# The last normalisation of a two-layer encoder: right half squared about its own mean, passes shared over three engines, three stores at the end

## The chip, the cores and the metric

The kernel runs on one core of a Trainium2 chip. A core has a matrix engine (TensorE, PE in the profile, with its weight loads as PEld), VectorE (DVE), ScalarE (ACT), GpSimd (POOL) and SyncE (SP), which here only issues transfers. Each engine works through its own instructions strictly in order and waits for others by semaphores. SBUF is the on-chip memory of 128 partitions; PSUM holds TensorE's sums. The metric is device time of one execution in microseconds (us).

## The reference

The input x is 1024 tokens by 1024 columns in float32. Two layers are computed: the first mixes tokens by latent attention, the second by differential attention, and each then has a gated feed-forward part. After each part stands a normalisation:

```python
h = _layernorm(ALPHA * h + mix, ln_mix_g[i], ln_mix_b[i])
h = _layernorm(ALPHA * h + _swiglu(h, ffn_w_gu[i], ffn_w_down[i]), ln_ffn_g[i], ln_ffn_b[i])

def _layernorm(x, g, b):
    mu = jnp.mean(x32, axis=-1, keepdims=True)
    var = jnp.mean(jnp.square(x32 - mu), axis=-1, keepdims=True)
    y = (x32 - mu) * lax.rsqrt(var + LN_EPS) * g + b
```

The change concerns the very last of these, behind the feed-forward part of the second layer, for the first 512 tokens.

## The kernel before, in words

Float32 products are made of three matmuls each on numbers split into a high and a low part: the cast to the high part is ScalarE's (`split`, the profile's L470), the subtraction for the low part VectorE's or GpSimd's (L471).

The second half of the function `ffn` multiplies the hidden activations with `w_dn`. It uses a scheme of seven products of half size in place of eight: the 1024 rows are two halves of four row blocks each (128 rows a block), the 1024 columns two halves (`lo_half`, `hi_half`). `whole` runs one of the seven products: 11 steps of the inner dimension, each for four row blocks, into four PSUM tiles of 128x512. `added` (L799) then adds such a PSUM tile to half a row block of `z`, on VectorE, and where it is the last addition to that half, it also leaves the row sums in `sums[block][:, 0]` (left half) or `[:, 1]` (right half).

The upper blocks 4 to 7 are complete after the fifth product and are normalised there by `finish`. The sixth product (`from_h(5, "7")`, `t3`) completes the right half of blocks 0 to 3. The seventh (`from_h(2, "4")`, `t4`) completes their left half; in the last layer (`next_x is None`) it runs blocks 0 and 1 together through the 11 steps, then block 2, then block 3. Its weights are made as it runs: VectorE subtracts (L770), ScalarE casts (L470), GpSimd subtracts (L471), TensorE uses them (L783).

Behind each block, `last(t)` adds the left half and calls `finish`, that is `layer_norm`: two one-column operations on VectorE make minus the mean from the two sums (L167, L168); ScalarE squares both halves of z about the mean and accumulates (L171), writing the squares to a PSUM tile that is free; VectorE forms (z - mean) * g over 1024 columns (L177); VectorE adds the two sums of squares and the epsilon (L179); GpSimd raises that to the power -1/2 (L181); VectorE forms y * rs + b over 1024 columns (L184), in halves for block 3; SyncE stores it (L185), 512 KB a block, two times 256 KB for block 3.

The instructions are written block by block; a compiler that simulates time puts them in the order in which each engine gets them, an earlier line first where several are ready. The small columns (means, sums, powers) come from one pool of 22 buffers (`small`). Nothing in the change is a matmul.

Of the kernel before, what the change touches and what calls it, by code (L numbers as in the profile page):

```python
# [11 lines left out]
AF = mybir.ActivationFunctionType  # L12
ALU = mybir.AluOpType
# [3 lines left out]
P = 128  # L17
S = 1024
D = 1024
# [11 lines left out]
LN_EPS = 1e-5  # L31
# [11 lines left out]
def trunk(  # L43
# [32 lines left out]
    nc = tc.nc  # L76
    V, A, G, T = nc.vector, nc.scalar, nc.gpsimd, nc.tensor
# [25 lines left out]
    mhalf = cst[:, 0:2]  # L103
# [22 lines left out]
    def small(name, n=1):  # L126
        return sp.tile([P, 2], F32, tag="small", name=name, bufs=22)[:, :n]
# [23 lines left out]
    def bcast_row(pool, src, n, name, tag):  # L151
        t = pool.tile([P, n], F32, tag=tag, name=name, bufs=1)
        nc.gpsimd.dma_start(t, src.partition_broadcast(P))
        return t
# [6 lines left out]
            reason="kept in program order",  # L161
        )

    def layer_norm(z, sums, junk, y, g, b, name, dst, n=1):

        nmu = small(f"nmu_{name}", 2)
        V.tensor_scalar(nmu[:, 0:1], sums[:, 0:1], sums[:, 1:2], -1.0 / (32 * D), ALU.add, ALU.mult)  # L167
        V.tensor_scalar(nmu[:, 1:2], sums[:, 0:1], sums[:, 1:2], -1.0 / D, ALU.add, ALU.mult)  # L168
        ssq = small(f"ssq_{name}", 2)
        squares = [  # L170
            A.activation(  # L171
                junk[i], z[:, i * 512:(i + 1) * 512], AF.Square,
                bias=nmu[:, 0:1], scale=1.0 / 32, accum_out=ssq[:, i:i + 1],
            )
            for i in range(2)
        ]
        centred = V.scalar_tensor_tensor(y, z, nmu[:, 1:2], g, ALU.add, ALU.mult)  # L177
        ve = small(f"ve_{name}")
        V.tensor_scalar(ve, ssq[:, 0:1], ssq[:, 1:2], LN_EPS, ALU.add, ALU.add)  # L179
        rs = small(f"rs_{name}")  # L180
        G.tensor_tensor(rs, ve, mhalf[:, 0:1], ALU.pow)  # L181
        for i in range(n):
            c = slice(i * D // n, (i + 1) * D // n)
            V.scalar_tensor_tensor(y[:, c], y[:, c], rs, b[:, c], ALU.mult, ALU.add)  # L184
            nc.sync.dma_start(dst[:, c], y[:, c])  # L185
        return squares[0].ins, centred.ins

    def to_xT(y, xT, tb, name, where):
# [90 lines left out]
    def out_proj(side, w_o, o_dram, x_src, x_dst, lng, lnb, xo):  # L279


        with tc.tile_pool(name="op0", bufs=2, side=side, reuse_waits="tile") as pool:
# [13 lines left out]
            for tb in LAST_ORDER:  # L296
                nm = f"a0_{tb}"
                of = pool.tile([P, H, P], F32, tag="of", name=f"of_{nm}", bufs=2)
                src = o_dram[tb // 2][:, :, (tb % 2) * P:(tb % 2) * P + P]
                nc.sync.dma_start(of, src.rearrange("h p q -> p h q"))  # L300
                ot = pool.tile([P, 2, D], F32R, tag="oh", name=f"oh_{nm}").rearrange("p a (h q) -> p a h q", h=H)
                oh, ol = ot[:, 0], ot[:, 1]
                A.copy(oh, of)
                V.tensor_tensor(ol, of, f32(oh), ALU.subtract)
                zy = pool.tile([P, 2, D], F32, tag="zy", name=f"zy_{nm}")
                z, y = zy[:, 0], zy[:, 1]
                nc.sync.dma_start(z, x_src[tb * P:(tb + 1) * P, :])
                sums = small(f"sum_{nm}", 2)
                junk = []
                for nh in range(2):  # L310
                    c = slice(nh * 512, nh * 512 + 512)
                    m = (ps_m if nh == 0 else ps_t)(f"zp_{nm}_{nh}")
                    junk.append(m)
                    mm3(m, [(oh[:, h, :], ol[:, h, :], wo[h][0][:, c], wo[h][1][:, c]) for h in range(H)])
                    V.scalar_tensor_tensor(
                        z[:, c], z[:, c], ALPHA, m, ALU.mult, ALU.add, accum_out=sums[:, nh:nh + 1]
                    )
                if tb == LAST_ORDER[-1]:
                    y = big_tile(f"y_{nm}", F32)[:, 0]
                layer_norm(z, sums, junk, y, g, b, nm, x_dst[tb * P:(tb + 1) * P, :])  # L320
                if prev is not None:
                    raw_x(prev[1], xo, prev[0], f"a0_{prev[0]}")
                prev = (tb, y)
        return lambda: raw_x(prev[1], xo, prev[0], f"a0_{prev[0]}")

    class OutProj:
# [90 lines left out]
        def rest(self, lng, lnb, xo):  # L417
            gb = big_tile("gb1", F32)
            for i, src in enumerate((lng, lnb)):
                nc.gpsimd.dma_start(gb[:, i], src.partition_broadcast(P))  # L420
            prev = None
            for tb in LAST_ORDER:
                if tb not in LAST_ORDER[:2]:
                    self.of(tb)
                if tb != LAST_ORDER[0]:
                    self.late(tb)
                z, y = self.z[tb]
                layer_norm(z, self.sums[tb], [self.m[tb, nh] for nh in range(2)], y, gb[:, 0], gb[:, 1],
                           f"a1_{tb}", self.x_dst[tb * P:(tb + 1) * P, :])
                if prev is not None:  # L430
                    raw_x(self.z[prev][1], xo, prev, f"a1_{prev}")
                prev = tb
            self.st.close()
            return lambda: raw_x(self.z[prev][1], xo, prev, f"a1_{prev}")
# [52 lines left out]
    def ffn(side, xo, xst, pending, layer, x_src, x_dst, lng, lnb, next_x):  # L487
# [3 lines left out]
        nm = f"f{layer}"  # L491
# [212 lines left out]
        z, sums = {}, {}  # L704
        lo_half, hi_half = slice(0, 512), slice(512, 1024)
# [74 lines left out]
        def step(o, h, w, tb, first, last):  # L780
            c = slice(tb * P, (tb + 1) * P)
            for a, b_ in ((0, 0), (0, 1), (1, 0)):
                T.matmul(  # L783
                    o, h[:, a, c], w[:, b_], start=(first and (a, b_) == (0, 0)), stop=(last and a == 1),
                    skip_group_check=True,
                )
# [7 lines left out]
        def rows(half, tb):  # L794
            return tb + 4 - 4 * half

        def added(half, cs, o, tb, acc=None, scale=1.0):
            n = rows(half, tb)
            banks_read.append(V.scalar_tensor_tensor(  # L799
                z[n][:, cs], z[n][:, cs], scale, o, ALU.mult, ALU.add,  # L800
                **({} if acc is None else {"accum_out": sums[n][:, acc:acc + 1]}),
            ).ins)

        def finish(tb, junk, y=None):
            y = z[tb] if y is None else y
            return layer_norm(z[tb], sums[tb], junk, y, g, b, f"{nm}_{tb}", x_dst[tb * P:(tb + 1) * P, :],
                              2 if next_x is None and tb == 3 else 1)

        def accumulators(name, tag):
            if tag == "x":  # L810
                return [ps_s(f"d{name}{layer}_{t}") for t in range(4)]
            return [(ps_m if t < 2 else ps_t)(f"d{name}{layer}_{t}") for t in range(4)]
# [8 lines left out]
        x4, y4 = accumulators("x", "x"), accumulators("y", "y")  # L821
# [3 lines left out]
        g = bcast_row(pool, lng, D, f"fg{layer}", "g")  # L825
        b = bcast_row(pool, lnb, D, f"fb{layer}", "b")
# [20 lines left out]
        y4 = accumulators("w", "y")  # L847
# [4 lines left out]
        x4 = accumulators("v", "x")  # L852
        whole(x4, from_h(6, "3"), block(1, hi_half, "b22"), True)
        for t in range(4):
            added(0, hi_half, x4[t], t, 1)
            finish(4 + t, [x4[t], x4[t]])

        whole(y4, from_h(5, "7"), t3(), False)
        for t in range(4):
            added(1, hi_half, y4[t], t, 1)  # L860

        def last(t):
            added(1, lo_half, y4[t], t, 0)
            finish(t, [y4[t], y4[t]])

        new, rest, normed = None, [], []
        if next_x is None:
            hs, ws = [], []
            for h, w in zip(from_h(2, "4"), t4()):
                hs.append(h)  # L870
                ws.append(w)
                for t in range(2):
                    step(y4[t], h, w, t, False, len(hs) == 11)
            stx.close()
            last(0)
            last(1)
            for t in range(2, 4):
                for j in range(11):
                    step(y4[t], hs[j], ws[j], t, False, j == 10)
                last(t)  # L880
        else:
# [11 lines left out]
            junk = wp.tile([P, 2, 512], F32, tag="wr", name=f"junk_{nm}", bufs=2)  # L893
            for t in range(4):
                y = yb[t // 2][:, t % 2]
# [4 lines left out]
            for t in range(4):  # L900
                y = yb[t // 2][:, t % 2]
# [133 lines left out]
    with ast as st:  # L1035
# [117 lines left out]
        for h in range(1, H):  # L1153
            b = 8 * (h - 1)
# [30 lines left out]
    xo, stacks = x_pools("m0", "right")  # L1185
    pending = out_proj("left", w_o_a, o_dr[0], x, xs_dr[0], ln_mix_g[0], ln_mix_b[0], xo)
    xT, rest, normed = ffn("left", xo, stacks, pending, 0, xs_dr[0], xs_dr[1], ln_ffn_g[0], ln_ffn_b[0], next_x)


    banks("ps3", PS_BUFS_B)  # L1190
    with ExitStack() as st:
# [11 lines left out]
        for ql in q_lo:  # L1203
            for mp in range(2):
                b = slice(64 - mp * 64, 128 - mp * 64)
                z = bb[b, :512]
# [132 lines left out]
        for h in range(1, H):  # L1339
            b = 8 * (h - 1)  # L1340
# [20 lines left out]
        b = 8 * (H - 1) - 2  # L1361
# [12 lines left out]
    pending = proj[0].rest(ln_mix_g[1], ln_mix_b[1], xo)  # L1374
    banks("ps4", PS_BUFS)
    ffn("right", xo, stacks, pending, 1, xs_dr[2], out, ln_ffn_g[1], ln_ffn_b[1], None)
    ps_stack.close()

# [87 lines left out]
```

## Time and profile before

| | |
|---|---|
| median of three runs | 2333.69 us |
| lowest and highest of them | 2331.33 and 2339.92 us |
| profiled execution, first to last instruction | 2331.5 us |
| TensorE busy | 2254.7 us |
| VectorE busy | 1556.9 us |
| ScalarE busy | 1017.4 us |
| GpSimd busy | 894.8 us |

The profiled execution has its span recorded, not a time of its own beside it; the lowest run is 0.1 us below that span and the median 2.2 us above it. In rows of the timeline the first number is the start in us from the span's start, the second the time from the first start to the last end of the instructions merged in that row, then engine, source line, operation, what is written and read, shapes and count; in brackets stands the idle time ahead and what ended it. In grouped rows the two numbers behind the bar are the total busy time in us and the mean of one instruction in ns. In rows with three numbers by slashes these are minimum, median and maximum in ns. A block's normalisation appears under the line numbers given above; `dw` is the PSUM tile of the last product, `wt` its weights.

### The profile page before, as it was taken

What the parts mean: (1) busy time and instruction counts of PE and PEld (TensorE: products, weight loads), DVE (VectorE), ACT (ScalarE), POOL (GpSimd) and SP (SyncE); (2) the same over time, 40 slices, a digit from 0 to 9 for tenths busy, and PEclk for the clock granted to TensorE, in tenths of its full rate; (3) what the DMA queues carried; (4) which work ended last, traced back from release to release, by engine and by line L of the source; (5) the groups of instructions that cost most, each with busy time, mean ns of one, the idle gap of its engine ahead of it and who ended that gap; (6) DMA issues with size and microseconds to landing.
All of it is one profiled execution on the core that took longest, in us unless ns stands there. A gap on an engine that the chain in (4) does not pass through costs nothing. (4 is left out here: it accounts for less than half of the span.)

```text
span 2331.5 us, 31115 instructions
## 1 busy us (share of the span) xinstructions
PE 2254.7 (97%) x11410; PEld 1918.7 (82%) x11410; DVE 1556.9 (67%) x2876; ACT 1017.4 (44%) x2089; POOL 894.8 (38%) x706
## 2 busy tenths in 40 slices
PE   7899999999999999999999999979999999999997
PEld 7898997888888887888888898867788888887885
DVE  4567664596656667677576666666596656658777
ACT  4366664352333333444465656545342333324353
POOL 3233452014444445555432424222014444436564
PEclk9999999999999999999999999989999999999999
DMA  5112324344323238454220212153334323337353
GB/s 201 35 57 89 120 90 161 109 163 153 118 85 131 73 118 320 172 194 153 91 55 19 69 37 69 37 190 101 124 141 151 107 98 106 111 131 303 142 203 118
DMA packets 102490, 288.29 MB, mean 124 GB/s; under 512 B 7856, under 2 KB 30000, under 8 KB 91840
## 3 DMA queue, kind: packets, MB, share of 16 engines
q1 hardware_dynamic: 96480, 267.48, 32.4%
q0 software_dynamic: 5856, 18.81, 2.5%
q8 instruction: 90, 1.47, 0.3%
q14 instruction: 64, 0.52, 0.1%
HBM read 205.00 MB, written 77.07 MB: 121 GB/s over the span
## 5 line engine op out<-in xcount | busy, mean ns | idle before, releaser
L470 ACT CAST op_g<-gr 128x512 fp32r<-128x512 f32 x240 | 147.5, 622 | 410.7 <-PE gb L515 228.1
L471 POOL TENSOR_TENSOR op_g<-gr,op_g 128x512 fp32r<-128x512 f32 x104 | 145.9, 1408 | 303.0 <-DVE tmp L606 153.6
L471 DVE TENSOR_TENSOR op_h<-rh,op_h 128x512 fp32r<-128x512 f32 x154 | 161.4, 1078 | 69.9 <-ACT op_h L470 69.9
L515 PE MATMUL ga<-xh_m,op_g 128*128 128x512 f32 x512 | 168.0, 389 | 0.0
L470 ACT CAST op_h<-rh 128x512 fp32r<-128x512 f32 x154 | 92.9, 619 | 147.7 <-PE dx L783 37.2
L783 PE MATMUL dw<-op_w_t,op_h 128*128 128x512 f32 x660 | 151.4, 390 | 0.2 <-DVE op_h L471 0.2
L783 PEld LDWEIGHTS dw<-op_w_t,op_h 128*128 128x128 f32 x660 | 123.6, 188 | 26.1 <-DVE op_h L471 0.6
L223 ACT ACTIVATE l_b<-l_b,mx_b 128x256 f32<-128x256 f32 (+7 forms) x128 | 99.6, 778 | 76.0 <-DVE mx_b L220 74.3
L1269 POOL TENSOR_SCALAR l_b<-l_b,r_b,cst 128x128 f32<-128x128 f32 (+3 forms) x64 | 52.8, 825 | 204.0 <-DVE r_b L225 194.8
L471 POOL TENSOR_TENSOR op_w_t<-tt,op_w_t 128x512 fp32r<-128x512 f32 x66 | 98.7, 1499 | 78.7 <-ACT op_w_t L470 76.8
L783 PE MATMUL dx<-op_w_b,op_h 128*128 128x512 f32 x528 | 122.6, 391 | 5.9 <-ACT op_w_b L470 3.9
L783 PEld LDWEIGHTS dx<-op_w_b,op_h 128*128 128x128 f32 x528 | 98.4, 188 | 29.8 <-ACT op_w_b L470 4.7
L515 PE MATMUL gb<-t4h_f,op_g 128*128 128x512 f32 x352 | 115.8, 390 | 3.2 <-DVE tmp L598 3.2
L515 PE MATMUL gc<-b22h_f,op_g 128*128 128x512 f32 x352 | 115.6, 389 | 1.0 <-ACT op_g L470 1.0
L471 DVE TENSOR_TENSOR op_g<-gr,op_g 128x512 fp32r<-128x512 f32 x136 | 109.5, 806 | 9.0 <-ACT op_g L470 8.8
L515 PE MATMUL gc<-t1h_f,op_g 128*128 128x512 f32 x352 | 115.5, 389 | 0.0
L515 PE MATMUL gb<-t3h_f,op_g 128*128 128x512 f32 x352 | 115.2, 389 | 0.0
L515 PE MATMUL gb<-t2h_f,op_g 128*128 128x512 f32 x352 | 114.9, 389 | 0.0
L515 PEld LDWEIGHTS ga<-xh_m,op_g 128*128 128x128 f32 x512 | 96.1, 188 | 20.0
L471 POOL TENSOR_TENSOR op_g<-s,op_g 128x512 fp32r<-128x512 f32 x40 | 55.9, 1398 | 142.9 <-ACT op_g L470 142.9
L144 PE MATMUL bp<-xT_f,h_wb 128*128 128x512 f32 x256 | 103.0, 402 | 0.1
L146 PE MATMUL bp<-xT_f,l_wb 128*128 128x512 f32 x256 | 101.6, 397 | 0.0
(381 smaller groups left out, 6788.5 us busy)
## 6 DMA issues: line engine op xcount, KB each, us to landing
gr<-in_w_gu SPq DMA_DIRECT2D x44, 1024.0 KB, 6.6
rh<-h_dr SPq DMA_DIRECT2D x28, 1024.0 KB, 4.9
h_dr<-sh SPq DMA_DIRECT2D x22, 1024.0 KB, 4.9
h_dr<-hp SPq DMA_DIRECT2D x22, 768.0 KB, 4.1
tt<-in_w_dn SPq DMA_DIRECT2D x22, 512.0 KB, 7.6
rh<-h_dr SPq DMA_DIRECT2D x14, 768.0 KB, 4.4
z<-xs_dr SPq DMA_DIRECT2D x16, 512.0 KB, 10.0
rw_b<-in_w_dn SPq DMA_DIRECT2D x8, 1024.0 KB, 8.8
```

Source lines behind the costliest of these rows:

```text
L144: T.matmul(ps_out, lh, rh, start=(i == 0), stop=False)
L146: T.matmul(ps_out, ll, rh, start=False, stop=(i == n - 1))
L223: A.activation(l[:, :n], l[:, :n], AF.Exp, bias=mx, scale=-1.0, accum_out=sm)
L470: A.copy(hi, src)
L471: eng.tensor_tensor(lo, src, f32(hi), ALU.subtract)
L515: T.matmul(o, w[:, a, kc], x[b][:, k, :], start=(first and k == 0 and (a, b) == (0, 0)), stop=(k == 3 and a == 1), skip_group_check=True,)
L783: T.matmul(o, h[:, a, c], w[:, b_], start=(first and (a, b_) == (0, 0)), stop=(last and a == 1), skip_group_check=True,)
L1269: G.tensor_scalar(l1[:, :n], l1[:, :n], r1, nlam, ALU.mult, ALU.mult)
```

## The change

Only the first four row blocks of the last layer's second normalisation are computed otherwise, by `begin_norm` and `end_norm` in place of `finish`.

`begin_norm(t)`, behind the sixth product: one column operation makes minus the mean of the right half alone, ScalarE squares the right half about that mean with a sum, and another column operation adds epsilon to it. `end_norm(t)`, behind the seventh product: ScalarE squares the left half about the same value (the right half's mean); from the two row sums VectorE forms minus the full mean and minus the square of the difference between the full mean and the right half's, with which the sum of squares is corrected to be about the full mean; GpSimd's power follows. For blocks 0 to 2, ScalarE then forms rs * z - rs * mean over 1024 columns, VectorE multiplies by g, GpSimd adds b, and SyncE stores. For block 3, VectorE forms (z - mean) * g in two halves ahead of the power, and y * rs + b in three pieces of 512, 256 and 256 columns behind it, each with its own store; the middle one is issued by ScalarE. `layer_norm` loses its splitting into `n` pieces, which only block 3 used.

```diff
-    def layer_norm(z, sums, junk, y, g, b, name, dst, n=1):
+    def layer_norm(z, sums, junk, y, g, b, name, dst):
...
-        for i in range(n):
-            c = slice(i * D // n, (i + 1) * D // n)
-            V.scalar_tensor_tensor(y[:, c], y[:, c], rs, b[:, c], ALU.mult, ALU.add)
-            nc.sync.dma_start(dst[:, c], y[:, c])
+        V.scalar_tensor_tensor(y, y, rs, b, ALU.mult, ALU.add)
+        nc.sync.dma_start(dst, y)
...
+        def square(t, i, cs, junk):
+
+            A.activation(
+                junk, z[t][:, cs], AF.Square, bias=about[t][0], scale=1.0 / 32, accum_out=about[t][1][:, i:i + 1]
+            )
+
+        def begin_norm(t, junk):
+
+
+            nb, q = small(f"nb{layer}_{t}"), small(f"q{layer}_{t}")
+            about[t] = nb, small(f"sq{layer}_{t}", 2), q
+            V.tensor_scalar(nb, sums[t][:, 1:2], -1.0 / (32 * 512), None, ALU.mult)
+            square(t, 1, hi_half, junk)
+            V.tensor_scalar(q, about[t][1][:, 1:2], LN_EPS, None, ALU.add)
+
+        def end_norm(t, junk):
+
+            s_lo, s_hi = (sums[t][:, i:i + 1] for i in range(2))
+            nb, sq, q = about[t]
+            square(t, 0, lo_half, junk)
+            d, nmu, rs = (small(f"{k}{layer}_{t}", 2) for k in ("dm", "nm", "rs"))
+            V.tensor_scalar(nmu[:, 0:1], s_lo, s_hi, -1.0 / D, ALU.add, ALU.mult)
+            V.tensor_scalar(d[:, 0:1], s_lo, s_hi, 1.0 / D, ALU.subtract, ALU.mult)
+            V.tensor_scalar(d[:, 1:2], d[:, 0:1], d[:, 0:1], -1.0, ALU.mult, ALU.mult)
+            V.tensor_scalar(d[:, 1:2], d[:, 1:2], q, None, ALU.add)
+            y, dst = z[t], x_dst[t * P:(t + 1) * P, :]
+
+            def scale():
+                V.tensor_scalar(rs[:, 1:2], sq[:, 0:1], d[:, 1:2], None, ALU.add)
+                G.tensor_tensor(rs[:, 0:1], rs[:, 1:2], mhalf[:, 0:1], ALU.pow)
+
+            if t < 3:
+                scale()
+                V.tensor_scalar(nmu[:, 1:2], nmu[:, 0:1], rs[:, 0:1], None, ALU.mult)
+                A.activation(y, y, AF.Identity, bias=nmu[:, 1:2], scale=rs[:, 0:1])
+                V.tensor_tensor(y, y, g, ALU.mult)
+                G.tensor_tensor(y, y, b, ALU.add)
+                nc.sync.dma_start(dst, y)
+                return
+            for cs in (lo_half, hi_half):
+                V.scalar_tensor_tensor(y[:, cs], y[:, cs], nmu[:, 0:1], g[:, cs], ALU.add, ALU.mult)
+            scale()
+            for cs, eng in ((lo_half, nc.sync), (slice(512, 768), nc.scalar), (slice(768, 1024), nc.sync)):
+                V.scalar_tensor_tensor(y[:, cs], y[:, cs], rs[:, 0:1], b[:, cs], ALU.mult, ALU.add)
+                eng.dma_start(dst[:, cs], y[:, cs])
...
         for t in range(4):
             added(1, hi_half, y4[t], t, 1)
+            if next_x is None:
+                begin_norm(t, x4[t])
 
         def last(t):
             added(1, lo_half, y4[t], t, 0)
-            finish(t, [y4[t], y4[t]])
+            end_norm(t, y4[t])
```

More of the change, by code (lines that the diff above doesn't have):

```diff
@@ L805, in finish @@
             y = z[tb] if y is None else y
-            return layer_norm(z[tb], sums[tb], junk, y, g, b, f"{nm}_{tb}", x_dst[tb * P:(tb + 1) * P, :],
-                              2 if next_x is None and tb == 3 else 1)
+            return layer_norm(z[tb], sums[tb], junk, y, g, b, f"{nm}_{tb}", x_dst[tb * P:(tb + 1) * P, :])
+        about = {}
+        def square(t, i, cs, junk):
+            A.activation(
+                junk, z[t][:, cs], AF.Square, bias=about[t][0], scale=1.0 / 32, accum_out=about[t][1][:, i:i + 1]
+            )
```

## The prediction

> **What bounds the kernel now.** I read the page first, to see which engine fills the span, then the chain that ended last, then the last 47 us engine by engine.
>
> ```profile
> span 2331.5 us, 31115 instructions
> ...
> PE 2254.7 (97%) x11410; PEld 1918.7 (82%) x11410; DVE 1556.9 (67%) x2876; ACT 1017.4 (44%) x2089; POOL 894.8 (38%) x706
> ```
>
> TensorE is the bound of the whole. The change touches nothing ahead of the last seventh product of the second feed-forward layer, so the question is where TensorE ends and what comes behind it. From the timeline of all engines:
>
> ```profile
> 2290.53 28.90 PE L783 MATMUL dw<-wt,op_h 128*128 128x512 f32 x126 [1.78 <-DVE z L799]
> ```
>
> The last product ends at 2290.53 + 28.90 = 2319.43, without a gap. What is left is a tail of 2331.46 - 2319.43 = 12.0 us, 0.52% of the time. A measurement of this kernel tells about 0.5%, 11.7 us, from no change: the tail would have to vanish for a visible gain. The chain of waits over the end, and the stretches by engine (busy us of PE, weight loads, VectorE, ScalarE, GpSimd, then clock and DMA):
>
> ```profile
> 2319.79 0.69 DVE z L799 x2
> 2320.47 1.20 DVE z L177
> 2321.67 0.14 DVE ve_f L179
> ...
> 2321.88 0.55 POOL rs_f L181
> ```
>
> ```profile
> 2309.50:2319.50 10.00, 9.93 (x44) 7.88 (x42) 7.64 (x18) 4.66 (x11) 1.10 (x2) 1.00 0.14 55
> 2319.50:2327.20 7.70, 0.00 (x0) 0.00 (x0) 6.56 (x12) 1.87 (x6) 1.09 (x2) 0.78 0.33 136
> ```
>
> Behind TensorE's end VectorE is busy 6.56 of 7.70 us: it is the bound of the tail, with GpSimd's power between two of its passes. VectorE's own timeline shows what it does there and what a pass costs:
>
> ```profile
> 2289.79 0.68 DVE L799 SCALAR_TENSOR_TENSOR z<-z,dw 128x512 f32<-128x512 f32 x1
> ...
> 2291.60 0.68 DVE L799 SCALAR_TENSOR_TENSOR z<-z,dw 128x512 f32<-128x512 f32 x1
> ...
> 2309.49 0.69 DVE L799 SCALAR_TENSOR_TENSOR z<-z,dw 128x512 f32<-128x512 f32 x1 [3.49 <-PE dw L783]
> ...
> 2310.79 0.21 DVE L167 TENSOR_SCALAR nmu_f<-fs 128x1 f32<-128x1 f32 x1
> 2310.91 0.20 DVE L168 TENSOR_SCALAR nmu_f<-fs 128x1 f32<-128x1 f32 x1
> ...
> 2312.73 1.28 DVE L177 SCALAR_TENSOR_TENSOR z<-z,nmu_f,fg 128x1024 f32<-128x1024 f32 x1 [1.61 <-ACT dw L171]
> ...
> 2314.71 0.69 DVE L799 SCALAR_TENSOR_TENSOR z<-z,dw 128x512 f32<-128x512 f32 x1 [0.33 <-PE dw L783]
> ...
> 2325.72 1.41 DVE L184 SCALAR_TENSOR_TENSOR z<-z,rs_f,fb 128x512 f32<-128x512 f32 x2 [0.66 <-POOL rs_f L181]
> ```
>
> A whole row block's pass is 1.28 us, the next one starting 1.20 later (chain); a half is about 0.60, and by the same proportion a quarter 0.32, an estimate. A one-column operation takes 0.2 and the next starts after 0.12. The last pass ends at 2327.13. Blocks 0 and 1 are released by TensorE at 2309.4, block 2 at 2314.7 and block 3 at 2319.4.
>
> **The change part by part.** First, the right half's squares. Four squares and eight one-column operations move ahead of the last product; only the left half's square stays behind each block's end.
>
> ```profile
> L171 ACT ACTIVATE dw<-z,nmu_f 128x512 f32<-128x512 f32 x8 | 5.5, 692 | 12.1 <-DVE nmu_f L167 11.9
> ...
> L171 ACT ACTIVATION_READ_ACCUMULATOR dw<-z,nmu_f 128x1 f32 x8 | 1.5, 187 | 0.0
> ```
>
> ```profile
> 2288.53 1.66 ACT L470 CAST op_h<-rh 128x512 fp32r<-128x512 f32 x3 [7.12 <-DMA rh<-h_dr]
> 2292.93 1.83 ACT L470 CAST wt<-rw_t 128x512 fp32r<-128x512 f32 x3 [2.75 <-DVE rw_t L770]
> ```
>
> ```profile
> 2293.63 14.77 POOL L471 TENSOR_TENSOR wt<-rw_t,wt 128x512 fp32r<-128x512 f32 x9 [11.64 <-ACT wt L470]
> ```
>
> One square with its read-out is 0.88 us. ScalarE has the gap from 2290.19 (2288.53 + 1.66) to 2292.93 for them, but the last right half is only added at 2291.60 + 0.68 = 2292.28. With the bias behind it, the last square starts at 2292.4 to 2292.8 and ends at 2293.3 to 2293.7, so the cast of 2292.93 slips by 0.4 to 0.7; I take 0.6. GpSimd's nine subtractions follow that cast without a gap, so their end slips alike, from 2308.40 (2293.63 + 14.77). Is there slack on TensorE? Block 0 is ready at 2309.45, 1.05 us behind the last subtraction; its three last matmuls start 0.23 apart (28.90 over 126) and one lasts 0.39 by this row, together about 0.85 to 0.95 us:
>
> ```profile
> L783 PE MATMUL dw<-wt,op_h 128*128 128x512 f32 x132 | 30.5, 391 | 3.3 <-DVE z L799 3.3
> ```
>
> That leaves 0.1, so I price this part at **+0.5 us**. Its bounds are 0 (squares put behind the casts, into ScalarE's later gaps) and +3.5 (all four, 4 x 0.88, ahead of the first cast).
>
> Second, blocks 0 to 2 get other passes. VectorE loses one of its two 1024-wide passes per block and keeps one (times g); ScalarE gets one of 1024 columns in place, with scale and bias from memory; GpSimd gets the addition of b. No row shows these three as they will be. The nearest: ScalarE at 1024 columns with a bias column and as a plain cast, and GpSimd over two 1024-wide inputs (minimum, median, maximum in ns):
>
> ```profile
> L223 ACT ACTIVATE l_b<-l_b,mx_b 128x1024 f32<-128x1024 f32 x16 | 18.4, 1152 | 21.4 <-DVE mx_b L220 21.4
> ```
>
> ```profile
> L303 ACT CAST oh_a<-of_a x8: 1045/1046/1056, 364.5 to 444.9; 128x1024 fp32r<-128x1024 f32 x8
> ```
>
> ```profile
> L138 POOL TENSOR_TENSOR l_pwo<-r_pwo,h_pwo x8: 2357/2404/2407, 101.2 to 311.8; 128x1024 fp32r<-128x1024 f32 x8
> ```
>
> I take 1.15 for ScalarE (bounds 1.05 and, another pointer by the same difference, 1.25) and 2.40 for GpSimd, twice VectorE's 1.28. The two do not run freely beside each other. VectorE's weight subtraction and GpSimd's, alone (minimum) and side by side (maximum):
>
> ```profile
> L770 DVE TENSOR_TENSOR rw_t<-rw_t,tt x9: 685/1776/1786, 2292.2 to 2302.5; 128x512 f32<-128x512 f32 x9
> ```
>
> ```profile
> L471 POOL TENSOR_TENSOR wt<-rw_t,wt x9: 1290/1740/1741, 2293.6 to 2307.1; 128x512 fp32r<-128x512 f32 x9
> ```
>
> Beside GpSimd the same VectorE operation is 1.09 us longer, so a 512-wide GpSimd operation shuts it out for 1.09 of its 1.29 us. At 1024 columns I take 2.40 - 0.20 = 2.20 us, an estimate. An operation that reads PSUM and one tile, or one column, I take as not shut out; no row shows it beside GpSimd (if it is, each costs up to 2.2 us more, once for block 3). The Trainium skill, SBUF — State Buffer, section "SBUF: two separate sides", says that a VectorE operation with two SBUF inputs and a GpSimd operation hold the shared ports exclusively, for the whole instruction. The trace agrees but for 0.2 us an operation; by the rule three additions would take 0.6 us more than in my sum, which would end at 2334.5.
>
> So the ports, and not VectorE, carry the tail. What they have to do from the first pass on: three additions 6.60, three products with g 3.60, for block 3 two half passes 1.20 and the last three 0.60 + 0.32 + 0.32: 12.64 us. The first pass starts when block 0 has gone through add (2309.49 to 2310.17), left square 0.88, the sum of squares 0.2, GpSimd's power 0.55, -mean times it 0.2 and ScalarE's pass 1.15, with 0.05 to 0.1 between engines: about 2313.55, against 2312.73 now. The floor for the last pass is 2313.55 + 12.64 = 2326.2, or 0.9 ahead of now.
>
> The order on the in-order queues decides what is lost on top, and no row fixes it, since the instructions are ordered by the compiler. I follow one plausible order, oldest block first, with each power going to GpSimd ahead of the next block's addition. Product 0: 2313.55 to 2314.75. Add of block 2: to 2315.4. Addition 0 holds the ports to 2317.0, product 1 to 2318.2, addition 1 to 2320.4. Power 2 fits between 2317.2 and 2318.2; its scaling on VectorE waits behind product 1, ScalarE's pass 2 is done at 2319.6, product 2 at 2321.6. Block 3 is added at 2319.45 and its left square done at 2321.0, all under addition 1. Its first half pass starts at 2321.6 before addition 2 is signalled, addition 2 holds 2322.2 to 2324.4 and ends at 2324.6, the second half pass at 2325.0. The power of block 3 is queued behind addition 2 and after the half passes: 2325.25 to 2325.8. The last three passes end at 2327.1, against 2327.13: **0.0 us**. The waits that are new: VectorE behind the power (behind it the next product), ScalarE behind that (behind it the next block's square), and GpSimd's addition behind the product, with the next power behind it.
>
> Third, the stores. The last pass's store is 128 KB instead of 256, and the one before it leaves by ScalarE's queue, which has nothing else then.
>
> ```profile
> out_dram<-z SPq DMA_DIRECT2D x4, 512.0 KB, 2.6
> ...
> out_dram<-z SPq DMA_DIRECT2D x2, 256.0 KB, 2.0
> ```
>
> By 0.6 us for 256 KB, 128 KB less saves 0.3; bounds 0 (the start is all that counts) and 0.6. SyncE's issues (0.99 for two, 2326.50 in the row below, the wait for the second pass within) come no closer than the passes:
>
> ```profile
> 2326.50 0.99 SPq L185 DMA_DIRECT2D out_dram<-z  x2
> ```
>
> ScalarE's own issue has no row; I take it like SyncE's. The stores of blocks 0 to 2 leave later than now, but the last of them at 2324.6 with 2.6 us to land, 2327.2, ahead of block 3's. What follows the landing, to 2331.46, stays. Edits to the other layers' normalisation (a loop of one turn removed) cost nothing, with no cover needed.
>
> **Sum.** +0.5 + 0.0 - 0.3 = +0.2 us on this execution's 2331.5, hence 2331.7. The runs shown are 2331.33 to 2339.92 with a median of 2333.69, 2.2 above the profiled span, so the forecast for a median is 2333.9: **no change that can be told**.
>
> **The rivals.**
>
> *GpSimd becomes the bound (slower).* If power 2 stands behind addition 1 on GpSimd's queue, it runs at 2320.6 instead of 2317.2. Then scaling, ScalarE's pass 2 to 2322.55, product 2 to 2323.8, addition 2 to 2326.25, power 3 to 2326.8, the last three passes to 2328.1: +1.0, with the first and third part +1.2, or 2334.9. It decides as soon as block 2's sum of squares is issued on VectorE behind product 1. For it: GpSimd's additions are the longest operations there and the two meet within a microsecond. Against it: GpSimd is free when product 1 holds the ports. The Trainium skill, GPSIMD Engine Reference, section 4.1 "Engine selection", advises VectorE for elementwise work, GpSimd being about twice as slow on two inputs; the rows above (2.40 against 1.28) agree, and this rival is what the rule would make of it.
>
> *The ports are kept dense (faster).* If power 3 goes ahead of addition 2, only the floor of 2326.2 counts: -0.9, with stores -0.3 and squares that hide in ScalarE's gap, -1.2, or 2332.5. For it: VectorE's half of the passes does go away, and powers are short. Against it: VectorE must then take block 3's sum of squares ahead of its half passes, which stand before it in the program.
>
> *The squares do not move.* If the order puts them behind the casts, ScalarE does them in its waiting time before 2311, where it was idle; the product is not delayed and the tail is as forecast: -0.3, or 2333.4.
>
> *The squares stall the product.* All four ahead of the cast, each waiting on VectorE: +3.5 and the rest as forecast, +3.2, or 2336.9.
>
> **How the numbers follow.** Forecast 0.40, GpSimd as bound 0.25, dense ports 0.17, squares not moved 0.10, stalled product 0.04; 0.04 for an order of the last 45 us that none of these describes. All priced cases lie within 3.2 us, against a bound of 11.7. A visible gain needs the tail to vanish, which the ports' 12.6 us exclude, so 0.02 for faster is only a measurement that strays; 0.05 for slower, the unpriced case and a stray; 0.93 for the same. For the range, three runs of before spread over 8.6 us; half of it, 4.3, is laid around the cases: 2332.5 - 4.3 = 2328.2 below; above, 2336.9 + 4.3 = 2341.2, of which I take 2341 since the stalled product is rare.
>
> **What would show it.** First part: the last product's matmul group ends later than 28.9 us after its start, and the weight casts start after 2293 with squares before them. Second: GpSimd rows of 128x1024 at 2.4 us or more in the tail, VectorE's products longer than 1.28 where they meet one, and the power of block 2 ahead of or behind addition 1. Third: a last store of 128 KB that lands in about 1.7 us. The forecast is wrong if the span behind TensorE's end is under 10.8 or over 13.5 us, if TensorE's last product slips by over 1 us, or if anything before 2286 us differs, for which the change gives no reason.

## The result, and the profile after

| | before | changed |
|---|---|---|
| median of 13 runs each | 2333.42 us | 2338.65 us |
| lowest to highest | 2328.51 to 2339.92 | 2337.74 to 2342.55 |
| profiled execution, span | 2331.5 us | 2336.9 us |

The ratio is 1.0029 with a 95% interval of 1.0020 to 1.0038: the changed kernel is slower by 0.29%, that is by 6.8 us with 4.7 to 8.9 as its interval. That lies within the 0.5% that the forecast called no change, but it is clear of zero, and it is many times the +0.2 us of the forecast's sum.

The order of the instructions on every engine is the same in both kernels up to the first right-half addition behind the sixth product. What differs in the spans ahead of that point (it stands at 2286.31 us before and at 2283.15 changed) belongs to the single execution. So I compare lengths from there on. The page of the changed kernel, then its timeline at the start of the last product (L797 is the addition that was L799, L468 the cast that was L470, L810 the square, L819 and L821 the two new one-column operations):

```profile
span 2336.9 us, 31144 instructions
...
PE 2255.2 (97%) x11410; PEld 1920.6 (82%) x11410; DVE 1553.7 (66%) x2894; ACT 1021.1 (44%) x2092; POOL 900.9 (39%) x709
```

```profile
2285.82 1.14 ACT L468 CAST op_h<-rh 128x512 fp32r<-128x512 f32 x2 [7.59 <-DMA rh<-h_dr]
...
2287.26 0.69 ACT L810 ACTIVATE dv<-z,nb 128x512 f32<-128x512 f32 x1 [0.30 <-DVE nb L819]
...
2288.10 0.15 DVE L821 TENSOR_SCALAR q<-sq 128x1 f32<-128x1 f32 x1 [0.28 <-ACT dv L810]
2288.17 0.68 DVE L797 SCALAR_TENSOR_TENSOR z<-z,dw 128x512 f32<-128x512 f32 x1
...
2290.41 0.15 DVE L821 TENSOR_SCALAR q<-sq 128x1 f32<-128x1 f32 x1 [0.88 <-ACT dv L810]
2290.48 0.68 DVE L797 SCALAR_TENSOR_TENSOR z<-z,dw 128x512 f32<-128x512 f32 x1
...
2292.24 0.15 DVE L821 TENSOR_SCALAR q<-sq 128x1 f32<-128x1 f32 x1 [0.88 <-ACT dv L810]
2292.31 0.68 DVE L797 SCALAR_TENSOR_TENSOR z<-z,dw 128x512 f32<-128x512 f32 x1
...
2296.00 23.87 PE L781 MATMUL dw<-wt,op_h 128*128 128x512 f32 x104 [0.38 <-POOL wt L469]
```

Ahead of the additions for blocks 2 and 3 VectorE now stands still 0.88 us each, because the one-column operation `q`, which needs ScalarE's square, is in its queue ahead of the next addition. Block 3's addition starts 2292.31 - 2285.82 = 6.49 us after the first cast behind the late transfer; before it was 2291.60 - 2288.53 = 3.07. The weights of the last product are made behind that addition, and TensorE ends at 2296.00 + 23.87 = 2319.87, 34.05 us after that cast, against 30.90 before: **+3.15 us**. The row at 2296.00 says what it waited for last: the first of these weights, 0.38 us.

The same timeline behind the last product (L843 is the product with g, L844 GpSimd's addition of b, L836 the sum of squares, L837 the power, L841 the scaling of the mean, L842 ScalarE's pass, L851 block 3's last passes):

```profile
2317.75 2.38 POOL L844 TENSOR_TENSOR z<-z,fb 128x1024 f32<-128x1024 f32 x1 [2.25 <-DVE z L843]
2317.83 3.38 DVE L843 TENSOR_TENSOR z<-z,fg 128x1024 f32<-128x1024 f32 x1
...
2321.29 2.34 POOL L844 TENSOR_TENSOR z<-z,fb 128x1024 f32<-128x1024 f32 x1 [1.16 <-DVE z L843]
...
2321.69 0.21 DVE L836 TENSOR_SCALAR rs<-sq,dm 128x1 f32<-128x1 f32 x1
...
2323.59 1.00 POOL L837 TENSOR_TENSOR rs<-rs,cst 128x1 f32<-128x1 f32 x1
...
2325.25 0.20 DVE L841 TENSOR_SCALAR nm<-nm,rs 128x1 f32<-128x1 f32 x1
...
2325.55 1.24 ACT L842 ACTIVATE z<-z,nm,rs 128x1024 f32<-128x1024 f32 x1 [2.20 <-DVE nm L841]
2326.00 1.54 DVE L851 SCALAR_TENSOR_TENSOR z<-z,rs,fb 128x512 f32<-128x512 f32 x3 [0.54 <-POOL rs L837]
...
2327.46 1.22 DVE L843 TENSOR_TENSOR z<-z,fg 128x1024 f32<-128x1024 f32 x1
2328.76 2.34 POOL L844 TENSOR_TENSOR z<-z,fb 128x1024 f32<-128x1024 f32 x1 [2.79 <-DVE z L843]
2331.12 0.33 SPq L845 DMA_DIRECT2D out_dram<-z  x1
```

Read it backwards. The last store is block 2's, not block 3's. Its addition of b waited for its product with g, which stood behind block 3's last passes on VectorE; its scaled mean stood there behind block 3's half passes and sum of squares; its power stood on GpSimd behind block 1's addition; its sum of squares stood on VectorE behind block 1's product, which GpSimd's addition for block 0 stretched to 3.38 us. That product held VectorE's queue: from 2317.83 to 2321.13 no other operation starts there, not even a one-column one. By stretches (as in the prediction's view), the last three of the changed kernel:

```profile
2319.87:2327.50 7.63, 0.00 (x1) 0.00 (x0) 6.88 (x18) 2.05 (x3) 4.10 (x4) 0.68 0.33 137
2327.50:2331.20 3.70, 0.00 (x0) 0.00 (x0) 1.18 (x2) 0.00 (x0) 2.34 (x1) 0.50 0.39 142
2331.20:2336.90 5.70, 0.00 (x0) 0.00 (x0) 0.00 (x0) 0.00 (x0) 0.00 (x0) 0.50 0.22 92
```

The first stretch is what was 7.70 us before. The second, 3.7 us for block 2's last two passes with nothing beside them, is new. The third is 1.4 us longer than what followed the last pass before (2331.46 - 2327.13 = 4.33 us), and the size of the last store is not the reason. What ends the span is GpSimd. Each engine's program closes with DRAIN instructions. First GpSimd's last instruction before, then its DRAINs before and in the changed kernel (shortest, middle and longest in ns, then the first and last start; `POOLq` is GpSimd's sequencer):

```profile
2325.14 0.55 POOL L181 TENSOR_TENSOR rs_f<-ve_f,cst 128x1 f32<-128x1 f32 x1 [2.72 <-DVE ve_f L179]
```

```profile
L1462 POOLq DRAIN  x3: 46/93/5571, 2325.1 to 2331.2; - x3
```

```profile
L1509 POOLq DRAIN  x3: 46/102/7361, 2328.7 to 2336.6; - x3
```

Before, the long DRAIN ends at 2325.1 + 5.57 = 2330.7, 5.0 us behind GpSimd's last instruction, block 3's power. In the changed kernel it ends at 2328.7 + 7.36 = 2336.1, again 5.0 us behind the last one, block 2's addition. SyncE's own DRAINs, which follow its waits for the stores, begin earlier, at 2329.4 and 2333.8. In all twelve profiled executions of this document the span ends 5.77 or 5.78 us behind GpSimd's last instruction, but 4.2 to 8.2 us behind VectorE's last pass and 3.8 to 5.4 us behind the last store's issue. So the tail is as long as GpSimd's last instruction is late. Why the DRAIN takes these 5 us is not shown.

The tail from TensorE's end is 17.03 us against 12.03: **+5.0 us**. Together +8.2 us on the length that the change touches, inside the interval of the times.

### The profile page after: what moved, and what is told of

It reads as the page before. It is cut to its first block, busy times and chain, and to the rows that moved or that the text cites. A ratio compares the mean times of both kernels' runs of the same rounds, so it can differ in the third digit from the quotient of the medians.

```text
span 2336.9 us, 31144 instructions
## 1 busy us (share of the span) xinstructions
PE 2255.2 (97%) x11410; PEld 1920.6 (82%) x11410; DVE 1553.7 (66%) x2894; ACT 1021.1 (44%) x2092; POOL 900.9 (39%) x709
## 3 DMA queue, kind: packets, MB, share of 16 engines
q8 instruction: 90, 1.47, 0.3%
## 5 line engine op out<-in xcount | busy, mean ns | idle before, releaser
L468 ACT CAST op_g<-gr 128x512 fp32r<-128x512 f32 x240 | 147.5, 622 | 410.9 <-PE gb L513 230.2
L468 ACT CAST op_h<-rh 128x512 fp32r<-128x512 f32 x154 | 93.1, 619 | 151.4 <-PE dx L781 39.8
```

What stands on the lines that cost most here:

```text
L468: A.copy(hi, src)
```

## The experiments

Three lengths are read in each run: from the first cast behind the late transfer to block 3's right-half addition ("to add 3"), from that cast to TensorE's end ("to end"), and from there to the end of the span ("tail"). "GpSimd's last" is the part of the tail from TensorE's end to the end of GpSimd's last instruction. "Pause" is TensorE's wait ahead of the group that starts once block 1's right-half addition is done. All starts are from the timelines.

| run | to add 3 | pause | to end | GpSimd's last | tail | span |
|---|---|---|---|---|---|---|
| before | 3.07 | 1.78 | 30.90 | 6.26 | 12.03 | 2331.5 |
| changed | 6.49 | 3.31 | 34.05 | 11.23 | 17.03 | 2336.9 |
| changed_again | 6.49 | 2.03 | 34.05 | 11.22 | 17.02 | 2336.4 |
| q_late | 4.19 | 3.07 | 33.09 | 11.36 | 17.16 | 2342.3 |
| no_early_squares | 3.08 | 1.02 | 30.86 | 10.69 | 16.44 | 2335.5 |
| vector_passes | 6.49 | 4.07 | 34.85 | 6.86 | 12.68 | 2337.5 |
| block2_vector | 4.20 | 1.63 | 31.76 | 8.45 | 14.25 | 2333.0 |
| b_on_vector | 4.20 | 3.41 | 32.96 | 7.76 | 13.51 | 2334.7 |
| power_first | 4.20 | 4.25 | 33.14 | 9.81 | 15.63 | 2340.3 |
| three_stores | 3.07 | 0.92 | 30.86 | 6.27 | 12.06 | 2329.2 |
| gap_squares | 3.08 | 3.54 | 32.42 | 5.32 | 11.09 | 2331.9 |
| gap_squares_again | 3.08 | 1.00 | 30.86 | 5.34 | 11.09 | 2335.7 |

The spans vary by what happens ahead of the last product and tell little; the lengths repeat to 0.01 or 0.02 us where a kernel was profiled twice, except where the pause differs. The spans are rounded to 0.1 us, so a tail is good to 0.05.

**q_late.** The epsilon is added behind the seventh product: the operation leaves `begin_norm` and stands in `end_norm` behind the left half's square.

```diff
-            V.tensor_scalar(q, about[t][1][:, 1:2], LN_EPS, None, ALU.add)
...
             square(t, 0, lo_half, junk)
+            V.tensor_scalar(q, sq[:, 1:2], LN_EPS, None, ALU.add)
```

> Only the one-column operation that adds epsilon to the right half's sum of squares moves, from behind the sixth product to behind the seventh. Two lengths are read: the product (from the start of block 0's right-half addition to the end of TensorE's last group: 33.1 us before, 36.7 changed) and the tail (from there to the end of the span: 12.0 before, 17.0 changed). Theory A, VectorE waits in its queue for ScalarE's squares between the additions: product 33.1 to 33.7. Rival B, the squares themselves delay ScalarE's weight casts: product stays at 36 or more. Rival C, the half clock that TensorE's pause sets off: it goes with the pause, so 33 to 34, but a lower clock would still be seen if the pause of over 3 us stayed. Tail by all of them 15.6 to 17.0, since block 2 is still last.

ScalarE's and TensorE's rows at the start of the product, and the clock (seventh column) in its first 7 us and the rest:

```profile
2292.05 1.14 ACT L468 CAST op_h<-rh 128x512 fp32r<-128x512 f32 x2 [7.76 <-DMA rh<-h_dr]
...
2293.49 0.69 ACT L810 ACTIVATE dv<-z,nb 128x512 f32<-128x512 f32 x1 [0.30 <-DVE nb L819]
...
2294.21 0.60 ACT L468 CAST op_h<-rh 128x512 fp32r<-128x512 f32 x1
...
2294.71 30.43 PE L781 MATMUL dw<-wt,op_h 128*128 128x512 f32 x126 [3.07 <-DVE z L797]
```

```profile
2294.71:2301.71 7.00, 7.00 (x24) 5.69 (x25) 6.97 (x12) 4.18 (x9) 3.45 (x3) 0.76 0.01 2
2301.71:2325.14 23.43, 23.43 (x104) 19.08 (x102) 14.70 (x33) 8.54 (x15) 13.98 (x10) 1.00 0.01 1
```

The additions come 2.3 us sooner (4.19 instead of 6.49), so VectorE's wait for the squares is most of the delay, as theory A has it. But A's number failed: measured as it was stated, the product took 35.95 us, not 33.1 to 33.7. That is just under B's 36, and the clock of 0.76 behind a pause of over 3 us is what C allowed for, so this number alone parts none of the three. Two things remain. ScalarE's square of block 0 stands between two activation casts, and the third cast ends 1.1 us later than without it; this holds up VectorE's additions by the 1.1 us that 4.19 has above 3.07. And the transfer came late in this execution (the first cast 2.86 us after block 0's addition, 2.22 before), TensorE paused 3.07 us, and its clock was 0.76 for the next 7 us: its 126 matmuls took 30.43 us instead of 28.90. The tail of 17.16 is a little above the 17.0 that all three named.

**no_early_squares.** All squares behind the seventh product.

```diff
         for t in range(4):
             added(1, hi_half, y4[t], t, 1)
-            if next_x is None:
-                begin_norm(t, x4[t])
...
             added(1, lo_half, y4[t], t, 0)
+            begin_norm(t, x4[t])
             end_norm(t, y4[t])
```

> The right half's squares are also done behind the seventh product; the passes stay as changed. Theory A: product 33.1, and what q_late has above this run is the price of the three squares in ScalarE's queue, 0 to 0.6. Rival B: only this run falls to 33.1, q_late does not. Tail: 15.6 to 18, since block 2 is still last through GpSimd; if early squares had been what gives the tail its length, under 15.

3.08 and 30.86, and as stated, from block 0's addition, 32.33 us against 33.1 (the transfer came 0.75 us sooner): the whole delay of the product hangs on what stands ahead of it. The tail is 16.44, so early squares are not what makes it long.

**vector_passes.** Blocks 0 to 2 by VectorE alone.

```diff
             if t < 3:
+                V.scalar_tensor_tensor(y, y, nmu[:, 0:1], g, ALU.add, ALU.mult)
                 scale()
-                V.tensor_scalar(nmu[:, 1:2], nmu[:, 0:1], rs[:, 0:1], None, ALU.mult)
-                A.activation(y, y, AF.Identity, bias=nmu[:, 1:2], scale=rs[:, 0:1])
-                V.tensor_tensor(y, y, g, ALU.mult)
-                G.tensor_tensor(y, y, b, ALU.add)
+                V.scalar_tensor_tensor(y, y, rs[:, 0:1], b, ALU.mult, ALU.add)
```

> Early squares and their one-column operations as changed; blocks 0 to 2 get back the two VectorE passes, none for ScalarE and GpSimd. Theory A: product still 36.7. Tail: if the sharing of the passes makes it long, 11 to 12.3; the rival, that the longer chain of one-column operations for each block makes it long, says 15 or more.

The tail falls from 17.03 to 12.68: the sharing of the passes makes it long, and not the one-column operations. It misses the 12.3 that I allowed. The product, as stated, took 38.28 us and not 36.7, with a pause of 4.07; its 6.49 to add 3 is the changed kernel's.

**block2_vector.** q_late, with only block 2 by VectorE alone.

```diff
-            if t < 3:
+            if t < 2:
...
+            if t == 2:
+                V.scalar_tensor_tensor(y, y, nmu[:, 0:1], g, ALU.add, ALU.mult)
+                scale()
+                V.scalar_tensor_tensor(y, y, rs[:, 0:1], b, ALU.mult, ALU.add)
+                nc.sync.dma_start(dst, y)
+                return
```

> As q_late, but block 2 too is normalised by VectorE alone; blocks 0 and 1 keep ScalarE's and GpSimd's passes. Product as q_late. Tail: if the length comes from block 2 being finished last through the chain of power, ScalarE, VectorE and GpSimd and its 512 KB store, 11.3 to 12.5; the rival, that GpSimd's additions of blocks 0 and 1 shut VectorE out for 2.2 us each and this is what is lost, says 14 or more.

14.25: neither alone. Against q_late 2.9 us go, so block 2's chain is the largest piece (its 512 KB store is no part of it: GpSimd's last instruction comes 2.91 us sooner); the rival's 14 or more holds too, since blocks 0 and 1 shared are still 1.6 us dearer than vector_passes. VectorE's rows show where: block 2's centring, an operation of 1.28 us alone, meets GpSimd's addition for block 0.

```profile
2316.90 3.31 DVE L848 SCALAR_TENSOR_TENSOR z<-z,nm,fg 128x1024 f32<-128x1024 f32 x1
```

The clock stayed full in this execution (pause 1.63), so its 31.76 to the end, against 30.86, prices early squares without VectorE's waits for them: +0.9 us.

**b_on_vector.** block2_vector, with b added by VectorE for blocks 0 and 1.

```diff
-                G.tensor_tensor(y, y, b, ALU.add)
+                V.tensor_tensor(y, y, b, ALU.add)
```

> As block2_vector (tail 14.25), but blocks 0 and 1 get b added on VectorE; ScalarE keeps its pass, GpSimd only has powers. If GpSimd's hold on the ports is what block2_vector's tail has above vector_passes' 12.68, the tail is 12.2 to 13.0; the rival, that ScalarE's pass and its waits are what is lost, says 13.8 or more.

13.51, between the two expectations. Of the 1.6 us, GpSimd's additions are 0.7 (8.45 to 7.76 in the column of GpSimd's last) and ScalarE's pass with its waits 0.9 (7.76 to 6.86).

**power_first.** q_late, with block 1's product and addition held until block 2's scaling is issued.

```diff
+                def passes(behind_=None):
+                    i = V.tensor_tensor(y, y, g, ALU.mult).ins
+                    if behind_ is not None:
+                        behind(i, behind_)
+                    G.tensor_tensor(y, y, b, ALU.add)
+                    nc.sync.dma_start(dst, y)
+                if t == 1:
+                    held.append(passes)
+                    return
+                if t == 2:
+                    held.pop()(scaled)
+                passes()
```

> As q_late, but block 2's sum of squares, power and scaling stand ahead of block 1's product with g and addition of b on VectorE and GpSimd; block 3's power stays behind block 2's addition, the order that the forecast assumed. If that order was the step that failed, the tail falls from 17.2 to 12 or 13. If GpSimd's additions bound the tail in any order, with VectorE shut out meanwhile, it falls only to 14.5 to 16.

Power 2 now stands ahead of addition 1, as the forecast had it, and the tail is 15.63 us and not 12. Its end, all engines:

```profile
2327.10 2.78 POOL L848 TENSOR_TENSOR z<-z,fb 128x1024 f32<-128x1024 f32 x1 [1.54 <-DVE z L845]
...
2327.73 2.70 DVE L859 SCALAR_TENSOR_TENSOR z<-z,nm,fg 128x512 f32<-128x512 f32 x1
...
2331.64 2.34 POOL L848 TENSOR_TENSOR z<-z,fb 128x1024 f32<-128x1024 f32 x1 [1.76 <-DVE z L845]
...
2333.93 0.55 POOL L837 TENSOR_TENSOR rs<-rs,cst 128x1 f32<-128x1 f32 x1
2334.52 1.54 DVE L862 SCALAR_TENSOR_TENSOR z<-z,rs,fb 128x512 f32<-128x512 f32 x3 [2.58 <-POOL rs L837]
```

Block 3's half pass is shut out by the addition for block 1 (2.70 us for 0.75), block 2's product follows, then its addition, and block 3's power, now GpSimd's last instruction, comes behind that. The order is not the forecast's throughout: here product 1 waits for block 2's scaling, and both half passes of block 3 go ahead of product 2, where the forecast had them the other way round. So this reordering is worth 1.5 us of the 5; what the forecast's whole order would give is not shown.

**three_stores.** The kernel before with block 3's last passes and stores as changed.

```diff
+        cuts = ((slice(0, D), nc.sync),) if n == 1 else (
+            (slice(0, 512), nc.sync), (slice(512, 768), nc.scalar), (slice(768, 1024), nc.sync))
```

> The kernel before with one thing of the change: block 3's last passes and stores in pieces of 512, 256 and 256 columns, the middle store by ScalarE. From the last VectorE pass's end to the span's end it was 4.33 us; if the size of the last store counts, about 4.0 (the recorded estimate of -0.3), if only its start counts 4.3. The last pass itself may end 0.1 later for its extra instruction.

The last pass ends at 2324.98, 4.22 us ahead of the span's end, against 4.33. The extra instruction makes the passes 1.54 instead of 1.41. The tail is 12.06: nothing gained. Nothing could be gained: GpSimd's last instruction, block 3's power, comes 6.27 us behind TensorE's end, before 6.26, and the passes and stores behind that power run beside GpSimd's DRAIN. The transfers from issue to landing:

```profile
out_dram<-z SPq DMA_DIRECT2D x1, 256.0 KB, 2.0
out_dram<-z ACTq DMA_DIRECT2D x1, 128.0 KB, 2.1
out_dram<-z SPq DMA_DIRECT2D x1, 128.0 KB, 2.0
```

**gap_squares.** Early squares without the waits: they are ordered behind the casts of the product's weights, `q` is added late, VectorE does all passes.

```diff
+                casts.append(A.copy(t[:, 0], r).ins)
...
+            behind(square(t, 1, hi_half, junk), casts[-1])
...
                     step(y4[t], h, w, t, False, len(hs) == 11)
+                if 5 <= len(hs) <= 8:
+                    begin_norm(len(hs) - 5, x4[len(hs) - 5])
```

> Early squares without the two waits: the right halves are squared behind the casts of the last product's weights (block 0 between two casts, blocks 1 to 3 behind the last), epsilon is added behind the product, all blocks are normalised by VectorE's two passes, and block 3 has three stores. Theory A (the waits on VectorE and ScalarE at the start of the product are the whole loss there): product 33.1 as before. Tail 11 to 12.3, against 12.0; total between 1 us faster than before and 0.5 slower, not told apart from before by its times. If early squares cost the product anything by themselves, over 34.

3.08 to add 3 again: without the two waits early squares do not delay the additions. TensorE had a pause of 3.54 us all the same (the transfer came 3.98 us after block 0's addition), and with it a granted clock of 0.50 from 2291 to 2293 us: 32.42 to the end, and 36.40 as stated, over the 34 that was to tell against theory A. That the reason lies outside the change is seen in gap_squares_again, below, where the pause is 1.00 and 30.86 to the end the same as without early squares. The tail is 11.09, 0.9 shorter than before. Its times: 2333.11 us against 2334.48, ratio 0.9996 (0.9983 to 1.0009): not told apart from before.

**changed_again and gap_squares_again.** Both kernels unaltered, a second time.

> The changed kernel once more, unaltered, to part what belongs to it from what a late transfer does. Theory A: from the first cast behind the late transfer to block 3's right-half addition 6.5 us again (before 3.1), whatever the transfer does; tail 17.0 again. TensorE's pause ahead of its main group and the length of that group vary: under 2 us the group's 126 matmuls run at full clock, over 3 us a stretch at half clock follows. If the 6.5 or the 17.0 move by over 0.5, they were an accident of one execution.

> gap_squares once more. Tail 11.1 again. From that cast to TensorE's end 30.9 if TensorE pauses under 2 us, 32.4 if over 3 us, as in the first look, since no wait of the change is left there. Its times: not told apart from before, or up to 0.1% faster; against the changed kernel's median 4 to 6 us faster.

6.49 and 17.02 repeat, and so does 34.05 to the end, with a pause of 2.03 instead of 3.31: in both executions of the changed kernel the late weights set TensorE's end, and not the pause. gap_squares_again had a pause of 1.00 and full clock:

```profile
2293.75 1.66 ACT L468 CAST op_h<-rh 128x512 fp32r<-128x512 f32 x3 [6.36 <-DMA rh<-h_dr]
...
2295.75 28.86 PE L782 MATMUL dw<-wt,op_h 128*128 128x512 f32 x126 [1.00 <-DVE z L798]
```

30.86 and 11.09, as expected. Its ratio to before is 0.9992 (0.9982 to 1.0002), its median 2333.18 us, 5.5 below the changed kernel's. It beats the changed kernel, whose ratio is 1.0020 to 1.0038; that it beats before is not shown.

## Why the prediction was right and wrong

The class, no change beyond 0.5%, and the range held, and so did the argument that a visible gain would need the whole tail of 12 us to vanish. The working did not hold. Two of the prediction's own signs of being wrong are there: the tail is 17.0 us where 13.5 was the most, and TensorE's end slipped 3.15 us where 1 was the most. The loss of 6.8 us is also beyond the dearest case priced, +3.2. That the median still lies inside the range owes to the 4.3 us laid around the cases for the scatter of before, which is luck as far as the mechanism goes. All three terms of the sum were off.

- *The right half's squares, +0.5.* Mis-sized: +3.15. The step looked at ScalarE's queue alone and let the squares slip one weight cast. It counted the second one-column operation of `begin_norm` on VectorE but not its wait, which puts a square between two additions. The rival "the squares stall the product" came near in mechanism and size (+3.5, all four squares; three stood ahead, block 3's ran behind the casts) with a chance of 0.04. The runs part it: additions 2.3 us earlier without that wait, another 1.1 without the squares between the casts.
- *The passes, 0.0.* This is the step that failed, and +5.0 came in its place. "I follow one plausible order, oldest block first" took block 2's sum of squares and block 3's addition as done under GpSimd's additions. Neither is shut out by itself, but on the chip both stood in VectorE's queue behind block 1's product, which was. Block 2 ends last. The rival "GpSimd becomes the bound" named the place, power 2 behind addition 1, and the condition, the sum of squares behind product 1; both are seen at 2321.69 and 2323.59. It priced them at +1.0, since it still let block 2's product go ahead of block 3's passes. By the runs' differences in GpSimd's last instruction the +5.0 are made up of -0.9 for early squares with their new chain of column operations (gap_squares against before), +1.5 mostly for blocks 0 and 1 being ready only 8.57 us ahead of TensorE's end instead of 9.94 (vector_passes against gap_squares; 37 matmuls start behind that point in place of 43), +0.9 for ScalarE's pass, +0.7 for GpSimd's two additions, +2.9 for block 2, and -0.1 for where the epsilon stands. The second of these was not in the forecast at all.
- *What ends the span.* The forecast counted to VectorE's last pass, then the store and its landing. Even in the kernel before that is not the path: GpSimd's last instruction is, with 5.77 us from its end to the end of the span. The forecast's order put that instruction 0.1 us later than before; on the chip it came 11.23 us behind TensorE's end instead of 6.26.
- *The shut-out on the ports, 2.2 us an addition.* Right: product 1 took 3.38 us beside GpSimd's addition where 1.22 is its length alone, 2.16 more. By the rule of the Trainium skill, SBUF — State Buffer, section "SBUF: two separate sides", that the ports are held for the whole instruction, it would be 2.30, an estimate: the product started at 2317.83 and the addition ended at 2317.75 + 2.38 = 2320.13. The trace agrees but for 0.14 us. That an addition from PSUM is not shut out held too: 0.68 us at 2321.82, under GpSimd's.
- *GpSimd's and ScalarE's passes.* 2.34 to 2.38 and 1.24 against 2.40 and 1.15.
- *The stores, -0.3.* Wrong: about 0, since the last store is not on the path (three_stores). Besides, a store of 128 KB lands in 2.0 us like one of 256 KB, and in the changed kernel the last store is 512 KB.

That the times moved by 6.8 us and not by 8.2 fits one more thing, which is argued and not shown: where the transfer comes late, the kernel before should lose 1.5 us to the half clock, as gap_squares did, while the changed kernel has that hidden under its late weights.

## What to carry to other kernels

A one-column operation that waits for another engine is as dear as that engine's work when it stands ahead of something urgent in an in-order queue; ask for each added instruction what is queued behind it, and put the reader of a result where it is needed, not where the result is made. Moving passes from a busy engine to a slower one that shares its way to memory moves the bound and adds latency to the block that comes last: leave the last blocks to the short chain. Ask which engine's end the span follows before shortening what seems to come last: here it was GpSimd's, and splitting the last store gained nothing. Whether a kernel that takes GpSimd out of the last block ends sooner was not run. Work that is to hide ahead of a product is best ordered into gaps that the trace shows.

## What was not expected of the hardware

The last product was profiled in twelve executions (one of the kernel before, two of the changed one, nine of variants). TensorE's clock was full after a pause of up to 1.78 us (five of them), and a stretch at half clock (0.50 granted) followed a pause of 2.03 us or more (seven). In each, another pause of 1.47 to 1.49 us and some 1.6 us of work stood ahead of that pause. Where nothing else bound it, the stretch cost about 1.5 us on 126 matmuls: 30.41 against 28.86 in the two executions of gap_squares. In changed_again the pause was only 2.03 us, and the clock was 0.78 in the 2 us behind it and 0.84 in the next 7:

```profile
2288.43:2290.44 2.01, 2.01 (x6) 1.11 (x6) 1.13 (x4) 0.81 (x2) 0.00 (x0) 0.78 0.09 37
2290.73:2297.73 7.00, 7.00 (x26) 5.53 (x27) 6.12 (x10) 3.26 (x6) 3.89 (x3) 0.84 0.00 1
```

The Trainium skill, TensorE: Matmul & The Clock Gate, section "HAM oscillation — how this bites in real kernels", sets the danger at idle gaps over about 3.4 us; here a pause of 2.03 us, with the one of 1.47 us ahead of it, was enough.
